# Row traffic of h on POOL's queue, row steps five or six units apart, scores of head pair 6 one unit sooner

## The chip, the cores and the metric

The kernel runs on one core of one Trainium2 chip. The time is the device time of one execution in microseconds, lower being better; the median of three runs is compared. A core has engines that run side by side, each with its own list of instructions in a fixed order: PE multiplies matrices into PSUM, DVE and ACT work on tiles element by element, POOL does a little of that and issues DMAs, and SP only issues DMAs. An instruction waits on semaphores for what it needs, and all that stands behind it on its engine waits too. That holds for DMA issues: what stands on SP behind an issue that waits is not issued.

## The reference

One layer over 256 latent tokens and 256 context tokens with 2048 channels, in float32. Both streams are normalised and modulated, projected by one wide matrix, and go through two branches:

```python
mod = jax.nn.silu(c) @ w_mod[l] + b_mod[l]
shift, scale, gate = jnp.split(mod[:, None, :], 3, axis=-1)
h = _layer_norm(x) * (1.0 + scale) + shift
h_c = _layer_norm(ctx) * (1.0 + scale_c) + shift_c
aq, ak, av, az, bq, bk, bv, bz, bg, mga, mgb = _split_cols(h @ w_in[l])
...
y_a = _neighborhood_attention(aq, ak, av, k_ctx, v_ctx, rpb[l])
y_b, y_b_c = _gla_mixer(bq, bk, bv, bg, bq_c, bk_c, bv_c, bg_c, ...)
out = _merge_branches(y_a, az, y_b, bz, mga, mgb, w_br_a[l], w_br_b[l], w_out[l])
x = _layer_norm(DEEPNORM_ALPHA * x + gate * out, ln_g[l], ln_b[l])
```

The first branch is attention over a window of 16 heads with 64 channels (eight pairs of heads). The second is a gated linear recurrence with four heads of 256 key channels and 512 value channels; the kernel computes it as attention weights of all tokens, multiplied by h, and then by the value weights.

## The kernel before

Each float32 operand of a product is split into two parts, hi and lo, of a shorter format, and a product takes three matmuls (hi with hi, lo with hi, hi with lo). ACT makes hi by a cast, DVE makes lo by a subtraction (`split`, L145). The weights come from HBM in units: one tile of 128 x 1024 (or 128 x 704 for the attention's values), fetched by SP into one of four buffers `raw` (`load`, L154), split into three pairs of buffers `hi` and `lo`, and then used by PE for 24 matmuls. `loads` counts the units, from the first after the start of the program. A call that is to be made at a unit stands in the table `events` under that unit's number; `load` makes it right after the split of that unit. That is how the attention's softmax, its transposes and the work on rows of h are laid between the units.

The program in order of time: about 137 us for the modulation, the normalised and transposed h (`hhi`, `hlo`) and the keys of head pairs 0 to 6 (`kp`). Then three groups of two head pairs: for each pair the query product (`qp`, 2 units), whose PSUM bank is emptied by L483, L484 and L487; then the values (`va`, 8 units of `av`, `value_columns`, L564), whose four PSUM banks are those that the query products of the group leave; beside them scores (`s`, L500), softmax and transposes (`tp`, L530) of both pairs. Then pairs 6 and 7, then keys and queries of the second branch (`bk`, `bq`), its gates (L641) and decays, then `attended` (L780) for two heads at a time, then the gates and output projections up to the end.

`attended` needs h again, with tokens on the partitions: h as rows, in the two parts. These rows, `hrows`, are made meanwhile and put in HBM, in eight blocks of 256 channels (`rows_of_h`, L396). For a block: fetch the modulation columns `sb` (512 KB out of `mods`, spread over all partitions) and the raw rows `xr` (four DMAs of 128 KB); scale them on DVE (eight instructions, L411 and L412); make the hi part in `sb` by ACT and the lo part in `xr` by DVE (`parts`); store both in `hrows`. Both tiles live in two buffers with the tag `staging`, which two more tiles of the second branch use later, `cs` and `wg` (L622, L623). So a block's fetch must wait until the block ahead is stored.

Before, all row DMAs are issued by SP, among the weights. Block n is fetched and scaled at unit 6 + 6n, made into parts a unit later, stored at unit 11 + 6n; the last step, block 7's, would be at unit 48, after `cs` and `wg` have been given the buffers, and so it is done in the first `attended`. POOL's queue carries the copies that bring keys and queries to the other half of the partitions (`kh` L477, `q` L488), and a few loads.

```python
for n in range(8):
    events.setdefault(6 + 6 * n, []).append(lambda dma, sub, n=n: rows_event(n, dma, sub))
```

Of the kernel before, what the change touches and what calls it, by code (L numbers as in the profile page):

```python
# [16 lines left out]
P = 128  # L17
# [11 lines left out]
NEG = -1.0e30  # L29
NC = 4  # L30
HELD = 4
SHARES = (
    ((0, 512, False), (512, 512, True), (1024, 512, False), (1536, 512, False)),
    ((0, 512, False), (512, 256, True), (1024, 512, False), (768, 256, True), (1536, 256, False), (1792, 256, False)),
# [54 lines left out]
def tile_backbone_layer(  # L89
# [34 lines left out]
    def k4(shape, name, dt=F32):  # L124
        return work.tile(shape, dt, tag="k4", name=name, bufs=4)
# [54 lines left out]
    def fetch(dst, src):  # L180
        with tc.issue_after(queued[-1]) if queued else nullcontext():
            queued.append(nc.sync.dma_start(dst, src).ins)
# [203 lines left out]
    def store_modulation():  # L386
        tp = bank("mdt")
        nc.tensor.transpose(tp[:64, :P], mds[:].rearrange("p a b k -> p (a b k)"), ident[:])
        mt = k2([64, P], "mdt")
        nc.vector.tensor_copy(mt[:], tp[:64, :P])  # L390
        nc.sync.dma_start(mods[:].rearrange("a b (k p) -> (a b k) p", p=P), mt[:])

    def staging(shape, name, dt=F32R):
        return const.tile(shape, dt, tag="staging", name=name, bufs=2)

    def rows_of_h(n):  # L396
        sb = staging([P, 2, 2, 256], f"sb{n}")
        xr = staging([P, 2, 4, P], f"xr{n}")
        b, x = sb[:].bitcast(F32), xr[:].bitcast(F32)
        cols = slice(256 * n, 256 * n + 256)  # L400

        def fetch_and_scale(dma, sub):
            with tc.issue_after(dma):
                nc.sync.dma_start(b, mods[:, :, cols].partition_broadcast(P))
                for i in range(4):
                    nc.sync.dma_start(x[:, :, i, :], xin[i, :, cols].rearrange("p (f c) -> p f c", f=2))
            for i in range(4):
                xi, s = x[:, :, i, :], i // 2
                scale, shift = (b[:, m, s, :].rearrange("p (f c) -> p f c", f=2) for m in range(2))
                with tc.issue_after(sub):  # L410
                    nc.vector.scalar_tensor_tensor(xi, xi, mvs[:, i, 0:1], scale, ALU.subtract, ALU.mult)  # L411
                nc.vector.scalar_tensor_tensor(xi, xi, rsn[:, 0, i : i + 1], shift, ALU.mult, ALU.add)  # L412

        def parts(dma, sub):
            with tc.issue_after(sub):
                split(
                    sb[:].rearrange("p a b c -> p (a b c)"),
                    xr[:].rearrange("p a b c -> p (a b c)"),
                    x.rearrange("p a b c -> p (a b c)"),
                )  # L420

        def store(dma, sub):
            with tc.issue_after(dma):
                for part, src in enumerate((b, x)):
                    nc.sync.dma_start(
                        hrows[2 * n : 2 * n + 2, :, part].rearrange("f p j c -> p f (j c)"),
                        src.rearrange("p f a b -> p f (a b)"),
                    )

        return fetch_and_scale, parts, store  # L430

    for n in range(8):
        events.setdefault(6 + 6 * n, []).append(lambda dma, sub, n=n: rows_event(n, dma, sub))

    def rows_event(n, dma, sub):
        fetch, parts, store = rows_of_h(n)
        fetch(dma, sub)
        events.setdefault(7 + 6 * n, []).insert(0, parts)
        events.setdefault(11 + 6 * n, []).insert(0, store)

    store_modulation()


    tri = k2([P, 2, P], "tri")
# [96 lines left out]
    def at(step, *calls):  # L541
        for fn, *args in calls:
            events.setdefault(step, []).append(lambda *_, fn=fn, args=args: fn(*args))
# [64 lines left out]
    f0, s0, t0 = attention(6, *first)  # L608
    f0()
    n = len(loads)  # L610
    at(n + 3, (s0, 0))
    at(n + 5, (s0, 1), (t0, 0))
    second = project_pair(7, q)
    f1, s1, t1 = attention(7, *second)
    at(n + 6, (f1,))
    at(n + 7, (s1, 0), (t0, 1))
    at(n + 9, (s1, 1), (t1, 0), (read_values, 6))
    at(n + 11, (t1, 1))
    at(n + 13, (read_values, 7))


    cs = staging([P, 3, T], "cs", F32)  # L622
    wg = staging([P, 2, 512], "wg")  # L623
    wr = k4([P, 2, 512], "wr")
    bgt = const.tile([P, NH, 2], F32, name="bgt")
    ngt = const.tile([P, 4], F32, name="ngt")
    for t, src in ((cs, rope), (wr, wg2), (bgt, bg2), (ngt, ng)):
        nc.gpsimd.dma_start(t[:], src)
    nc.scalar.copy(wg[:], wr[:])
    lo = slice(64, 128)  # L630
    nc.vector.tensor_tensor(out=wg[lo], in0=wr[lo], in1=wg[lo].bitcast(F32), op=ALU.subtract)
    def rope_of(dst, src, name, eng):
        t = k2([P, 2, T], f"rt_{name}")
        for a in range(2):
# [45 lines left out]
    def queries(h, room=acc):  # L680
        qf = k2([P, 2, T], f"qf{h}")
        for a in range(2):
            bp = room(f"bq{h}{a}")
            project_t(f"bq{h}{a}", bp[:, :T], T, xh, xl)
            nc.scalar.mul(qf[:, a, :], bp[:, :T], 1.0 / 16.0)
        return qf
# [155 lines left out]

    pws = [weights_of(0)]
    kf = keys(0)
    turn_gates()
    decays = gates(0)
    kq = kf, queries(0)
    parts = decayed(0, *decays, *kq)
    decays = gates(1)
    kq = keys(1), queries(1)  # L850
# [373 lines left out]
```

## Time and profile before

| | |
|---|---|
| median of 3 runs | 1245.19 us (1243.39 to 1246.96) |
| the profiled execution | 1247.71 us, of which the span from the first to the last instruction is 1246.0 us |
| mean granted clock of PE | 0.994 |
| DMA | 264.55 MB, mean 212 GB/s |
| queue of SP (q1) | 83744 packets, 252.53 MB |
| queue of POOL (q0) | 4736 packets, 10.37 MB |
| row DMAs | 8 of sb, 32 of xr, 16 of hrows, all issued by SP |

The page of the profile has engines' busy times and their shares of the span; lists of who waited for whom; and, on request, each engine's instructions in order of time. A row of that order has the start in us, the duration, the engine, the line, the tile written and the tile read, and in brackets how long the engine had been idle just ahead of it and what ended that. PE's matmuls overlap, so a start tells more than a duration.

### The profile page before, as it was taken

The numbers are of one execution on the slowest core, as the hardware profiler recorded it, in microseconds if no ns is written. First come the engines' busy times: TensorE is split into PE (matmuls) and PEld (weight loads), VectorE is DVE, ScalarE is ACT, GpSimd is POOL, SyncE is SP. The second block draws the span as 40 slices with busy tenths as digits, with TensorE's granted clock in tenths as the row PEclk, the third lists the DMA queues.
The fourth block names the chain that finished last, engine by engine and source line by source line (L and its number), as shares of the span: only waits on it lengthen the run. The fifth ranks groups of instructions, "written<-read, shape, count | busy, mean of one in ns | idle before, by whom it ended". The sixth has DMA issues, their size and how long they took to land.

```text
span 1246.0 us, 17116 instructions
## 1 busy us (share of the span) xinstructions
PE 1207.7 (97%) x6617; PEld 1015.1 (81%) x6617; DVE 757.5 (61%) x1114; ACT 536.9 (43%) x752; POOL 73.0 (6%) x106
## 2 busy tenths in 40 slices
PE   6999989999999999999999999999999999999997
PEld 5666889989788998888788898788888888888785
DVE  6755566666569376355543368898555554555577
ACT  4322445545456354253533364444444344444440
POOL 1000101010110101002000000000000000000111
PEclk9999989999999999999999999999999999999999
DMA  9997458787743434554645669989655556557661
GB/s 378 418 407 285 145 151 245 186 202 178 216 155 120 134 108 130 203 152 135 233 145 182 215 207 319 312 299 312 210 186 191 196 186 195 194 186 269 223 218 68
DMA packets 88993, 264.55 MB, mean 212 GB/s; under 512 B 9536, under 2 KB 22928, under 8 KB 83792
## 3 DMA queue, kind: packets, MB, share of 16 engines
q1 hardware_dynamic: 83744, 252.53, 60.3%
q0 software_dynamic: 4736, 10.37, 2.9%
q8 instruction: 52, 0.85, 0.3%
q10 hardware_dynamic: 432, 0.56, 0.1%
q14 instruction: 29, 0.24, 0.1%
HBM read 247.66 MB, written 10.52 MB: 207 GB/s over the span
## 4 chain that ended last, share of the span: by engine, by line
PE 70%; DMA 12%; DVE 10%; issue 3%; ACT 3%; SPq 2%; POOL 0%; DVEq 0%; ACTq 0%; POOLq 0%
PE bk L143 7%; PE mgb L143 7%; PE mga L143 7%; PE pb L143 7%; PE g L143 6%; PE o L143 6%; PE kp L143 6%; PE pa L143 3%; DMA wg<-in_wgate 3%; PE va L143 3%; PE bq L143 3%; PE wo L143 3%; PE az L143 2%; DMA hrows<-xr 2%; PE gp L143 2%
## 5 line engine op out<-in xcount | busy, mean ns | idle before, releaser
L149 DVE TENSOR_TENSOR l_wv<-r_wv,h_wv 128x1024 fp32r<-128x1024 f32 x32 | 39.2, 1225 | 79.8 <-ACT h_wv L147 79.6
L143 PE MATMUL o<-h_wv,gt 128*128 128x512 f32 x256 | 84.1, 391 | 0.6 <-DVE gt L149 0.6
L143 PE MATMUL g<-ah,hr 128*128 128x512 f32 x256 | 79.3, 390 | 1.1 <-DMA hr<-hrows 1.1
L143 PE MATMUL va<-h_av,hhi 128*128 128x352 f32 x192 | 64.5, 336 | 9.9 <-ACT q L487 9.9
L149 DVE TENSOR_TENSOR l_pb<-r_pb,h_pb 128x1024 fp32r<-128x1024 f32 x32 | 39.2, 1225 | 47.8 <-ACT h_pb L147 47.8
L147 ACT CAST h_wv<-r_wv 128x1024 fp32r<-128x1024 f32 x32 | 33.6, 1049 | 74.4 <-DMA r_wv<-in_wst 74.4
L143 PE MATMUL va<-h_av,hlo 128*128 128x352 f32 x192 | 63.0, 328 | 0.0
L143 PE MATMUL va<-l_av,hhi 128*128 128x352 f32 x192 | 62.9, 327 | 0.0
L149 DVE TENSOR_TENSOR l_mgb<-r_mgb,h_mgb 128x1024 fp32r<-128x1024 f32 x32 | 39.2, 1224 | 32.7 <-ACT h_mgb L147 32.5
L955 DVE SCALAR_TENSOR_TENSOR gacc<-wg,sc,gacc 128x512 f32<-128x512 f32 x64 | 46.4, 747 | 17.9 <-DMA wg<-in_wgate 17.5
L143 PEld LDWEIGHTS o<-h_wv,gt 128*128 128x128 f32 x256 | 47.8, 188 | 11.6 <-DVE gt L149 1.8
L149 DVE TENSOR_TENSOR l_mga<-r_mga,h_mga 128x1024 fp32r<-128x1024 f32 x32 | 39.1, 1223 | 28.9 <-ACT h_mga L147 28.9
L143 PEld LDWEIGHTS g<-ah,hr 128*128 128x128 f32 x256 | 47.7, 188 | 11.0 <-DMA hr<-hrows 1.3
L147 ACT CAST h_mga<-r_mga 128x1024 fp32r<-128x1024 f32 x32 | 33.8, 1055 | 49.5 <-PE mga L143 31.2
L143 PE MATMUL kp<-hhi,h_ak 128*128 128x512 f32 x128 | 52.7, 418 | 2.2 <-ACT hhi L304 2.2
L147 ACT CAST h_mgb<-r_mgb 128x1024 fp32r<-128x1024 f32 x32 | 33.6, 1054 | 47.7 <-PE mgb L143 26.1
L147 ACT CAST h_pb<-r_pb 128x1024 fp32r<-128x1024 f32 x32 | 33.7, 1053 | 43.4 <-PE pb L143 30.1
L143 PE MATMUL bz<-l_bz,hhi 128*128 128x512 f32 x128 | 50.1, 391 | 2.0 <-DVE l_bz L149 2.0
L143 PE MATMUL kp<-hhi,l_ak 128*128 128x512 f32 x128 | 51.7, 404 | 0.0
L304 ACT ACTIVATE hhi<-xt,mds 128x256 fp32r<-128x256 f32 x32 | 17.5, 594 | 78.8 <-DVE mds L298 78.8
L143 PE MATMUL bk<-hhi,h_bk 128*128 128x512 f32 x128 | 50.4, 394 | 0.7 <-ACT kf L675 0.7
L143 PE MATMUL kp<-hlo,h_ak 128*128 128x512 f32 x128 | 50.6, 398 | 0.0
(351 smaller groups left out, 3560.4 us busy)
## 6 DMA issues: line engine op xcount, KB each, us to landing
wm<-in_wmod SPq DMA_DIRECT2D x32, 1024.0 KB, 9.4
hr<-hrows SPq DMA_DIRECT2D x32, 512.0 KB, 4.3
r_wv<-in_wst SPq DMA_DIRECT2D x32, 512.0 KB, 3.6
r_bz<-in_wst SPq DMA_DIRECT2D x32, 512.0 KB, 4.9
wg<-in_wgate SPq DMA_DIRECT2D x64, 256.0 KB, 5.1
r_mga<-in_wst SPq DMA_DIRECT2D x32, 512.0 KB, 3.6
r_mgb<-in_wst SPq DMA_DIRECT2D x32, 512.0 KB, 3.3
r_pb<-in_wst SPq DMA_DIRECT2D x32, 512.0 KB, 3.3
```

Source lines behind the costliest of these rows:

```text
L143: return nc.tensor.matmul(o, a, b, start=start, stop=stop).ins
L147: cast = nc.scalar.copy(hi, src)
L149: sub = nc.vector.tensor_tensor(out=lo, in0=src, in1=hi.bitcast(F32), op=ALU.subtract)
L304: cast = nc.scalar.activation(hhi[:, s, kt, :], x, AF.Identity, scale=m, bias=b)
L955: nc.vector.scalar_tensor_tensor(part, raw[:], sc[:, n // 4, 0:1], part, ALU.mult, ALU.add)
```

## The change

All row DMAs, and the store of `mods`, are issued on POOL. The fetch of block 0 is issued as soon as `mods` is stored; that of block n + 1 right behind block n's stores, in the same step. The steps are a table, `ROW_STEPS`: scaling at units 6, 11, 17, 22, 27, 32, 37 and 42, parts and stores a unit later. The scaling stands behind the unit's subtraction on DVE without the order that `issue_after` forced. Block 7 is thus finished at unit 43, ahead of `cs` and `wg`, whose loads and splits move behind the first keys of the second branch; the queries of its head 0 are put ahead of its gates. The first scores of head pair 6 come a unit sooner (n + 2), the last transposes and the values of pair 7 a unit later.

```diff
+ROW_STEPS = (6, 11, 17, 22, 27, 32, 37, 42)
...
-        nc.sync.dma_start(mods[:].rearrange("a b (k p) -> (a b k) p", p=P), mt[:])
+        nc.gpsimd.dma_start(mods[:].rearrange("a b (k p) -> (a b k) p", p=P), mt[:])
...
-        def fetch_and_scale(dma, sub):
-            with tc.issue_after(dma):
-                nc.sync.dma_start(b, mods[:, :, cols].partition_broadcast(P))
-                for i in range(4):
-                    nc.sync.dma_start(x[:, :, i, :], xin[i, :, cols].rearrange("p (f c) -> p f c", f=2))
+        nc.gpsimd.dma_start(b, mods[:, :, cols].partition_broadcast(P))
+        for i in range(4):
+            nc.gpsimd.dma_start(x[:, :, i, :], xin[i, :, cols].rearrange("p (f c) -> p f c", f=2))
+
+        def scale(dma, sub):
             for i in range(4):
...
-        def store(dma, sub):
-            with tc.issue_after(dma):
-                for part, src in enumerate((b, x)):
-                    nc.sync.dma_start(
...
+            for part, src in enumerate((b, x)):
+                nc.gpsimd.dma_start(
+                    hrows[2 * n : 2 * n + 2, :, part].rearrange("f p j c -> p f (j c)"),
+                    src.rearrange("p f a b -> p f (a b)"),
+                )
+            if n + 1 < 8:
+                rows_of_h(n + 1)
+
+        events.setdefault(ROW_STEPS[n], []).append(scale)
+        events.setdefault(ROW_STEPS[n] + 1, []).insert(0, parts)
 
     store_modulation()
+    rows_of_h(0)
...
-    at(n + 3, (s0, 0))
+    at(n + 2, (s0, 0))
...
-    at(n + 11, (t1, 1))
-    at(n + 13, (read_values, 7))
+    at(n + 12, (t1, 1))
+    at(n + 14, (read_values, 7))
...
     pws = [weights_of(0)]
     kf = keys(0)
+    cs = staging([P, 3, T], "cs", F32)
+    wg = staging([P, 2, 512], "wg")
...
     turn_gates()
+    qf = queries(0)
     decays = gates(0)
-    kq = kf, queries(0)
+    kq = kf, qf
```

How this moves instructions is seen at three places. The first is SP's list at the values of the first group (r_av is a weight tile on its way into `raw`, rb the attention's bias), before:

```order
L156 DMA r_av_0_1440<-in_wav 128x704
L156 DMA r_av_2_1470<-in_wav 128x704
L404 DMA sb_1476<-mods 128x4x256
L406 DMA xr_1477<-in_xin 128x2x128 x4
L156 DMA r_av_4_1530<-in_wav 128x704
L156 DMA r_av_6_1562<-in_wav 128x704
L156 DMA r_av_8_1619<-in_wav 128x704
L497 DMA rb_1625<-in_rpb 128x768
```

and in the change:

```order
L157 DMA r_av_0_1447<-in_wav 128x704
L157 DMA r_av_2_1477<-in_wav 128x704
L157 DMA r_av_4_1530<-in_wav 128x704
L157 DMA r_av_6_1571<-in_wav 128x704
L157 DMA r_av_8_1628<-in_wav 128x704
L490 DMA rb_1634<-in_rpb 128x768
```

The row fetch no longer stands between the second and the third weight tile of the group.

The second is POOL's list in the third group, from the key copies of pair 5 to those of pair 6, before:

```order
L477 DMA kh_2490<-kn_2486 64x512
L477 DMA kh_2490<-kl_2487 64x512
L488 DMA q_2393<-q_2393 64x256 x4
L477 DMA kh_2980<-kn_2976 64x512 x2
L477 DMA kh_2980<-kl_2977 64x512 x2
```

and in the change, where sb_2312 and xr_2313 are block 4, sb_2553 and xr_2554 block 5, sb_2800 and xr_2801 block 6:

```order
L470 DMA kh_2499<-kn_2495 64x512
L470 DMA kh_2499<-kl_2496 64x512
L423 DMA hrows<-sb_2312 128x2x512
L423 DMA hrows<-xr_2313 128x2x512
L481 DMA q_2404<-q_2404 64x256 x2
L403 DMA sb_2553<-mods 128x4x256
L405 DMA xr_2554<-in_xin 128x2x128 x4
L481 DMA q_2404<-q_2404 64x256 x2
L423 DMA hrows<-sb_2553 128x2x512
L423 DMA hrows<-xr_2554 128x2x512
L403 DMA sb_2800<-mods 128x4x256
L405 DMA xr_2801<-in_xin 128x2x128 x4
```

The query copies of the group's two pairs now stand behind the stores of block 4 and behind the fetch of block 5.

The third is DVE's list at the first scores of pair 4 (s, its bias, its maximum nm, its sum sm and weights pr; xr is the row block's scaling, l_av the lo part of a weight tile), before:

```order
L149 TENSOR_TENSOR l_av_6_2719<-r_av_6_2716,h_av_6_2718 128x704
L508 TENSOR_TENSOR s_0_2645<-s_0_2645,rb_2566 128x2x256
L510 TENSOR_REDUCE nm<-s_0_2645 128x2
L517 RECIPROCAL sm<-sm 128x2
L522 TENSOR_SCALAR pr_0_2653<-pr_0_2653,sm 128x512
L149 TENSOR_TENSOR l_av_8_2776<-r_av_8_2773,h_av_8_2775 128x704
```

and in the change:

```order
L150 TENSOR_TENSOR l_av_6_2728<-r_av_6_2725,h_av_6_2727 128x704
L501 TENSOR_TENSOR s_0_2656<-s_0_2656,rb_2594 128x2x256
L412 SCALAR_TENSOR_TENSOR xr_2554<-xr_2554,mvs,sb_2553 128x2x128
L503 TENSOR_REDUCE nm<-s_0_2656 128x2
L413 SCALAR_TENSOR_TENSOR xr_2554<-xr_2554,rsn,sb_2553 128x2x128
L412 SCALAR_TENSOR_TENSOR xr_2554<-xr_2554,mvs,sb_2553 128x2x128 x2
L413 SCALAR_TENSOR_TENSOR xr_2554<-xr_2554,rsn,sb_2553 128x2x128
L510 RECIPROCAL sm<-sm 128x2
L413 SCALAR_TENSOR_TENSOR xr_2554<-xr_2554,rsn,sb_2553 128x2x128
L515 TENSOR_SCALAR pr_0_2664<-pr_0_2664,sm 128x512
L412 SCALAR_TENSOR_TENSOR xr_2554<-xr_2554,mvs,sb_2553 128x2x128
L150 TENSOR_TENSOR l_av_8_2793<-r_av_8_2790,h_av_8_2792 128x704
```

The scaling of block 5 now stands among the softmax of pair 4, ahead of its maximum.

More of the change, by code (lines that the diff above doesn't have):

```diff
@@ L420, in parts @@
                 )
-        def store(dma, sub):
-            with tc.issue_after(dma):
-                for part, src in enumerate((b, x)):
-                    nc.sync.dma_start(
[L426 to L439, printed above, removed]
+            for part, src in enumerate((b, x)):
[7 more added lines that the diff above has]
+        events.setdefault(ROW_STEPS[n] + 1, []).insert(0, parts)
     store_modulation()
+    rows_of_h(0)
     tri = k2([P, 2, P], "tri")
@@ L617, in tile_backbone_layer @@
     at(n + 9, (s1, 1), (t1, 0), (read_values, 6))
-    at(n + 11, (t1, 1))
-    at(n + 13, (read_values, 7))
[L622 to L631, printed above, removed]
+    at(n + 12, (t1, 1))
+    at(n + 14, (read_values, 7))
     def rope_of(dst, src, name, eng):
@@ L844, in tile_backbone_layer @@
     kf = keys(0)
+    cs = staging([P, 3, T], "cs", F32)
+    wg = staging([P, 2, 512], "wg")
+    wr = k4([P, 2, 512], "wr")
+    bgt = const.tile([P, NH, 2], F32, name="bgt")
+    ngt = const.tile([P, 4], F32, name="ngt")
+    for t, src in ((cs, rope), (wr, wg2), (bgt, bg2), (ngt, ng)):
+        nc.gpsimd.dma_start(t[:], src)
+    nc.scalar.copy(wg[:], wr[:])
+    lo = slice(64, 128)
+    nc.vector.tensor_tensor(out=wg[lo], in0=wr[lo], in1=wg[lo].bitcast(F32), op=ALU.subtract)
     turn_gates()
+    qf = queries(0)
     decays = gates(0)
-    kq = kf, queries(0)
+    kq = kf, qf
     parts = decayed(0, *decays, *kq)
```

## The prediction

> **What bounds the kernel now.** I read the page first, then who waited for whom on PE, then the order of time on SP, ACT, DVE and PE around each of PE's waits, and last the stages.
>
> The page's first part, and the list of PE's waits over the whole span (engine, line, what it waited for: us in total, times, longest):
>
> ```profile
> PE 1207.7 (97%) x6617; PEld 1015.1 (81%) x6617; DVE 757.5 (61%) x1114; ACT 536.9 (43%) x752; POOL 73.0 (6%) x106
> ...
> PE va L143 <- ACT q L487: 9.9, 3, 5.2
> ...
> PE s L143 <- ACT pr L514: 2.6, 1, 2.6
> ...
> PE g L143 <- DMA hr<-hrows: 1.1, 1, 1.1
> ```
>
> PE is the bound: 1207.7 of 1246.0 us, so only 38.3 us are idle. The change can win only what PE loses between the first row block (about 140 us) and the last (about 605 us): three waits of va, 9.9 us; one of s, 2.6; one of g, 1.1.
>
> The first va wait in order of time (start, us, engine and line; brackets: idle before and what ended it), on SP, ACT, DVE and PE:
>
> ```profile
> 144.57 0.44 SPq L404 DMA_DIRECT2D sb<-mods  x1
> 145.06 5.36 SPq L406 DMA_DIRECT2D xr<-in_xin  x4
> 150.51 2.67 SPq L156 DMA_DIRECT2D r_av<-in_wav  x3
> ...
> 158.38 0.78 ACT L147 CAST h_av<-r_av 128x704 fp32r<-128x704 f32 x1 [5.12 <-DMA r_av<-in_wav]
> 160.44 0.38 ACT L487 ACTIVATE q<-qp 64x256 fp32r<-64x256 f32 x1 [0.49 <-DVE q L484]
> ...
> 155.98 0.88 DVE L411 SCALAR_TENSOR_TENSOR xr<-xr,mvs,sb 128x256 f32<-128x256 f32 x2 [4.23 <-DMA xr<-in_xin]
> ...
> 160.87 0.66 PE L143 MATMUL va<-h_av,hhi 128*128 128x352 f32 x1 [5.16 <-ACT q L487]
> 161.33 0.49 PE L143 MATMUL va<-l_av,hhi 128*128 128x352 f32 x1
> 161.63 0.49 PE L143 MATMUL va<-h_av,hlo 128*128 128x352 f32 x1
> ...
> 170.04 0.32 PE L143 MATMUL va<-l_av,hhi 128*128 128x352 f32 x1
> 170.19 0.32 PE L143 MATMUL va<-h_av,hlo 128*128 128x352 f32 x1
> ```
>
> SP issues the row fetch (sb, four xr) ahead of the third weight tile r_av; the four xr take 5.36 us, so r_av leaves at 150.51 and lands about 158.4. ACT, which works in order, sits on its cast for 5.12 us, and the copies L487 that free the PSUM bank of the query product stand behind it, the last at 160.44: PE waits 5.16 us. The other two waits are the same story at the next two groups:
>
> ```profile
> 209.05 2.67 SPq L156 DMA_DIRECT2D r_av<-in_wav  x3
> ...
> 216.52 0.78 ACT L147 CAST h_av<-r_av 128x704 fp32r<-128x704 f32 x1 [5.81 <-DMA r_av<-in_wav]
> ...
> 265.37 1.92 SPq L156 DMA_DIRECT2D r_av<-in_wav  x3
> ...
> 272.69 0.78 ACT L147 CAST h_av<-r_av 128x704 fp32r<-128x704 f32 x1 [6.46 <-DMA r_av<-in_wav]
> ```
>
> A second loss is hidden in busy time. After the 5.2 us wait va matmuls start 0.30 us apart (161.33, 161.63); later 0.15 (170.04, 170.19). The stages of 40 us (PE, PEld, DVE, ACT, POOL busy; granted clock, DMA share, GB/s) show it as the clock:
>
> ```profile
> 160.00:200.00 40.00, 39.13 (x233) 38.07 (x234) 27.38 (x43) 20.49 (x38) 4.58 (x9) 0.91 0.65 183
> 200.00:240.00 40.00, 37.98 (x268) 35.55 (x267) 22.50 (x35) 18.41 (x35) 2.04 (x4) 1.00 0.66 178
> 240.00:280.00 40.00, 37.33 (x258) 34.92 (x257) 28.24 (x47) 19.48 (x36) 6.11 (x12) 0.96 0.88 221
> ```
>
> Lost: 9% and 4% of 40 us, 3.6 + 1.6 = 5.2 us.
>
> **The change part by part.**
>
> *Weights no longer behind rows on SP.* On SP the 57 issues of mods (1), sb (8), xr (32) and hrows (16) go; r_av tiles follow each other (order rows above). r_av can leave when its buffer is free, some 4 us sooner, and lands before ACT's cast. What is late next at the first place: DVE scales the rows with the query's subtractions among them, and from the first scaling (155.98) to the end of the last L487 (160.82) it was 4.8 us. DVE is free at 151.8 (its row of 150.86, below, and 0.89), so the last L487 ends at 156.6; PE stood from 155.7 (160.87 less 5.16): 0.9 us stay. At the other two places the row work moves away from the query's evacuation, or its data are fetched some five units sooner; I leave nothing there. So 9.9 - 0.9 = **9.0 us won**. The clock loss goes with its waits; I leave 1 us: 5.2 - 1.0 = **4.2 us**.
>
> *Row block 7.* Now it finishes before cs and wg take its buffers; before, it was served at 586 to 600 us and g waited on hrows: **1.1 us**, all won.
>
> *Scores of pair 6 a unit sooner.* The wait of 2.6 us was DVE standing on xr:
>
> ```profile
> 319.00 0.36 SPq L404 DMA_DIRECT2D sb<-mods  x1
> ...
> 329.26 0.91 DVE L411 SCALAR_TENSOR_TENSOR xr<-xr,mvs,sb 128x256 f32<-128x256 f32 x2 [3.60 <-DMA xr<-in_xin]
> ...
> 338.21 0.70 DVE L508 TENSOR_TENSOR s<-s,rb 128x512 f32<-128x512 f32 x1
> ```
>
> Now DVE treats s ahead of the row scaling, but xr7 stands before the next weights (l_bk); I take 1.6 of 2.6, **1.6 us won**.
>
> *At no cost.* The turns and values of pair 7 come a unit later, on PE between matmuls that have their weights; what reads them (the gated path, L842) is far off. cs and wr are fetched behind block 7's stores as they were behind block 6's.
>
> Won in all: 9.0 + 4.2 + 1.1 + 1.6 = **15.9 us**.
>
> *What the rows cost on POOL.* POOL's own work is small (73.0 us busy), so issue time is not the matter; the round of one block is, since block n+1 uses block n's two buffers. Its rows (count: min/median/max ns), issues (median us to landing), and a fetch with little beside it (block 7):
>
> ```profile
> L411 DVE SCALAR_TENSOR_TENSOR xr<-xr,mvs,sb x32: 462/479/486, 156.0 to 591.8; 128x256 f32<-128x256 f32 x32
> L147 ACT CAST sb<-xr x8: 1045/1048/1053, 161.0 to 592.9; 128x1024 fp32r<-128x1024 f32 x8
> L149 DVE TENSOR_TENSOR xr<-xr,sb x8: 1219/1224/1226, 162.0 to 594.7; 128x1024 fp32r<-128x1024 f32 x8
> ...
> hrows<-xr SPq DMA_DIRECT2D x8, 512.0 KB, 5.3
> ...
> wr<-in_wg POOLq DMA_DIRECT2D x1, 512.0 KB, 5.2
> ...
> r_bk<-in_wst SPq DMA_DIRECT2D x16, 512.0 KB, 3.7
> ...
> 585.96 1.92 SPq L406 DMA_DIRECT2D xr<-in_xin  x4
> ...
> 589.25 0.48 DVE L411 SCALAR_TENSOR_TENSOR xr<-xr,mvs,sb 128x256 f32<-128x256 f32 x1 [0.77 <-DMA xr<-in_xin]
> ```
>
> Scaling 8 x 0.48 = 3.8, cast 1.05, subtraction 1.2, store 5.3, and a fetch between 3.3 us (585.96 to 589.25, xr alone) and 10.3 (319.00 to 329.26, sb and xr behind other work on SP). That makes 14.7 to 21.7 us. The trace shows no row DMA on POOL; the nearest price of that queue is 512 KB in 5.2 us against 3.7 on SP, 1.5 more a hop, two hops a round: 17.7 to 24.7. I take a fetch of 8 us, between the ends since the queue is its own but the engines are shared (DMA share 0.65 to 0.88): a round of about 22.4.
>
> The time that PE gives for a round: from unit 6 to unit 42 DVE went in before from 150.86 to 324.44:
>
> ```profile
> 150.86 0.89 DVE L149 TENSOR_TENSOR l_av<-r_av,h_av 128x704 fp32r<-128x704 f32 x1 [1.31 <-ACT h_av L147]
> ...
> 324.44 1.22 DVE L149 TENSOR_TENSOR l_aq<-r_aq,h_aq 128x1024 fp32r<-128x1024 f32 x1 [3.56 <-ACT h_aq L147]
> ```
>
> 173.6 us, less the 9.9 and 5.2 lost there, 158.5 over seven gaps: 22.6 us a gap. The round just fits, with nothing to spare, and the gaps are uneven. The shortest is block 5: its store begins after step 28's subtraction, and DVE needs its data right behind s of pair 4 (order rows above: a scaling stands ahead of the nm of s). The two places before:
>
> ```profile
> 257.84 1.22 DVE L149 TENSOR_TENSOR l_aq<-r_aq,h_aq 128x1024 fp32r<-128x1024 f32 x1
> ...
> 278.44 0.70 DVE L508 TENSOR_TENSOR s<-s,rb 128x512 f32<-128x512 f32 x1
> ```
>
> Of these 20.6 us some 4 go (the third va wait and its slow clock), and scaling and subtraction (5.0) come in ahead of the store: some 11.5 are left, when store and fetch want 5.3 + 8, or 3.0 more. It is late by 2 to 5 us; PE has two units of va (24 x 0.16 us each, 7.7 us) before it needs that PSUM pair again, and the chain s, nm, exponentials takes half of these. I put 1.5 us there. The queries' copies q, which now stand behind hrows or sb on POOL, and the four kh, which wait for row DMAs landing, are needed within 10 us: 0.7 us. The gates of head 0, now after its queries, meet DVE later: 0.5 us. **Cost 2.7 us.**
>
> *Sum.* 15.9 - 2.7 = 13.2 us. The profiled execution took 1247.7 (1246.0 span, 1.7 around it): 1234.5 for such a one. It was 2.5 above the median of the three runs, 1245.2, so I forecast a median of **1232**.
>
> A rule that speaks against it: the Trainium skill, "SBUF — State Buffer", section "SBUF: two separate sides", says a DMA issued from GpSimd is starved while VectorE runs a copy that takes both ports, since its descriptors cannot be written; it names 3.1 us in place of 0.62. No row here shows that: POOL's own issues (count: min/median/max ns) are even, with VectorE busy 61%:
>
> ```profile
> L477 POOL DMA_DIRECT2D kh<-kl x16: 512/519/567, 141.1 to 337.8; - x16
> ```
>
> By that rule, an estimate, 2.5 us on each of two hops a round would make the round 27.4 and the time about 1263; by the row it adds nothing, and I go by the row, with a chance for the rival below.
>
> **The rivals.**
>
> *Rows come early.* With a fetch of 5 us or less the round is 19.4, all waits of the cost part go, and of s nothing is left: 15.9 + 1.0 = 16.9 off, and part of the 1.9 left at the first wait and the clock: median 1227. For it: block 7's 3.3 us. Against: DMA share up to 0.88 there, and block 7's row traffic is added to the same stretch.
>
> *Same transfers, same wait.* The weights share the 16 engines with the rows on whatever queue; r_av lands as late as before, or DVE stands on late rows. The round at 24.7 costs (24.7 - 22.6) x 7 = 14.7 of the 15.9: about 1244. For it: DMA share 0.65 to 0.88 where the waits are. Against: r_av was not slow on the engines, it left late (150.51), behind 5.36 us of issues. The Trainium skill, "DMA: Bandwidth & Descriptors", "Issuing engines are not separate DMA queues", says that another issuing engine saves only issue time; the row shows that issue time is just what was lost here.
>
> *Slower.* Row issues on POOL are held up by DVE or by landing waits in one file: POOL issues in order, so q and kh of the next scores stand behind hrows, which stands behind DVE. If each of seven issues of a round is stretched by one DVE copy (0.68 us, the kT copy below), the round is 22.4 + 4.8 = 27.2, and 7 x 4.6 = 32 us are lost against 15.9 won: 1261; at 26 it is 1253. It decides from a round of 24.9 (22.6 + 15.9 / 7).
>
> ```profile
> 139.50 0.68 DVE L458 COPY kT<-kp 128x512 f32<-128x512 f32 x1
> ```
>
> For it: such copies run all through the attention part. Against: the even 512 to 567 ns.
>
> **How the numbers follow.** Forecast 1232 (1228 to 1238): 0.55. Rows early, 1227: 0.20. Same transfers, 1240 to 1248: 0.14. Slower, 1250 to 1262: 0.11. The range leaves out the slower rival and the edge of the third: 1225 to 1246. Faster and slower are counted from 0.3% (3.7 us), about what a measurement can tell: below 1241.5, forecast, early rows and a little of the third, 0.77; above 1248.9, 0.11; between, 0.12.
>
> **What would show it.** In the profile after: va waits on L487 of at most 2 us in all, and a granted clock of 0.98 or more in 160:280 (first terms). ACT's wait for r_av gone; if it is still 5 us, the third rival. DVE's wait for xr: up to 10 us in all if my round is right, near none if rows are early, over 25 if they are slow. No wait of g on hr. The longest new PE wait at s or tp of pair 4 or 5. POOL's issues of xr near 0.5 us; over 1 us, the slower rival. The prediction is wrong if PE's idle between 140 and 620 us does not fall by at least 6 us.

## The result and the profile after

| | before | after |
|---|---|---|
| median | 1245.07 us (6 runs, 1243.39 to 1247.16) | 1251.86 us (6 runs, 1250.58 to 1253.52) |
| after / before | | 1.0054, 95% interval 1.004 to 1.0068 |
| span of the profiled execution | 1246.0 us | 1250.8 us |
| mean granted clock | 0.994 | 0.990 |
| POOL's queue (q0) | 10.37 MB, 2.9% of the 16 engines' time | 27.19 MB, 9.6% |

The change makes the kernel slower by half a per cent; the forecast was a gain of one. PE's waits from 140 to 620 us in the profile after (engine, line, what it waited for: us in total, times, longest):

```profile
PE s L144 <- DMA q<-q: 9.1, 2, 7.5
PE va L144 <- ACT q L480: 7.6, 2, 6.6
PE s L144 <- DVE xr L413: 3.0, 1, 3.0
PE qp L144 <- DVE low L573: 1.7, 1, 1.7
```

Two of the three va waits have all but gone, but the longest has grown from 5.2 to 6.6 us. The wait of s for the softmax weights (2.6) has become two waits for the query's copy (9.1), and two waits are new: s behind the row scaling, and qp behind DVE's emptying of the value banks. In all PE is idle for 23.0 of the 480 us from 140 to 620, where it was idle for 16.6 before. The stages show what the clock takes besides (columns as in the prediction):

```profile
160.00:200.00 40.00, 37.40 (x221) 36.35 (x222) 28.80 (x48) 20.90 (x40) 12.76 (x19) 0.91 0.78 195
...
240.00:280.00 40.00, 39.79 (x284) 37.66 (x283) 25.82 (x40) 20.48 (x37) 16.53 (x26) 1.00 0.99 227
280.00:320.00 40.00, 35.36 (x225) 33.97 (x224) 28.23 (x50) 20.38 (x37) 8.56 (x13) 0.96 0.68 192
320.00:360.00 40.00, 30.94 (x169) 24.75 (x169) 19.45 (x29) 14.26 (x27) 10.02 (x17) 0.87 0.72 185
```

The loss of 240:280 is cured; that of 160:200 stays, and 280:360 is new. ACT's last copy of the second branch's keys says how far PE is behind, before and after:

```profile
573.20 0.59 ACT L675 COPY kf<-bk 128x512 f32<-128x512 f32 x1 [4.34 <-PE bk L143]
```

```profile
584.35 0.59 ACT L658 COPY kf<-bk 128x512 f32<-128x512 f32 x1 [4.34 <-PE bk L144]
```

It is 11.2 us behind there, and 4.8 at the end of the span: the wait of g for hr (1.1) is gone, as are those of o on DVE (0.6) and of bz on its weights (2.0). These are 3.7 of the 6.4 us made up; the rest was not traced.

**The first place.** SP issues no rows any more, and the weight tiles are late all the same (SP, ACT, DVE and PE, each in order of time):

```profile
144.48 5.26 SPq L157 DMA_DIRECT2D r_av<-in_wav  x3
...
156.75 0.78 ACT L148 CAST h_av<-r_av 128x704 fp32r<-128x704 f32 x1 [6.48 <-DMA r_av<-in_wav]
...
158.73 0.78 ACT L148 CAST h_av<-r_av 128x704 fp32r<-128x704 f32 x1 [0.80 <-DMA r_av<-in_wav]
...
158.37 0.87 DVE L412 SCALAR_TENSOR_TENSOR xr<-xr,mvs,sb 128x256 f32<-128x256 f32 x2
...
162.60 0.66 PE L144 MATMUL va<-h_av,hhi 128*128 128x352 f32 x1 [6.60 <-ACT q L480]
```

These are the second, third and fourth weight tile of the group, issued within 5.3 us, and ACT still sits 6.48 us before its cast of the second, which it had not waited for before. The third left at 146.87 in place of 150.51, and ACT has it at 158.73, no sooner than before (158.38). What the transfers took says why. For r_av between 143 and 165 us, before and after:

```profile
DMA to landing us min/median/max: 4.3/7.3/7.8
```

```profile
DMA to landing us min/median/max: 5.1/12.0/12.2
```

And in the stage 144:148 the 16 DMA engines are busy for 0.94 of the time while they move 74 GB/s (last two columns); in 160:200 they moved 195 at 0.78:

```profile
144.00:148.00 4.00, 4.00 (x36) 4.00 (x35) 1.85 (x3) 1.63 (x3) 1.03 (x2) 1.00 0.94 74
```

That is the time of the fetch of sb, which now leaves at 139.78, some 5 us sooner than before (144.57), and lands 11.7 us later. Busy engines that move little are the clue that the experiments followed. It is not the only way in which such a fetch shows: before, with the same fetch on SP's queue, the engines were busy for only 0.26 of the stage 148:152, while SP's four xr issues stretched over 5.36 us:

```profile
148.00:152.00 4.00, 4.00 (x36) 4.00 (x35) 2.21 (x3) 2.09 (x5) 1.03 (x2) 1.00 0.26 88
```

**Block 5 and pair 6.** The fetch of block 5 on POOL, DVE's first scaling of it, and PE's wait behind that:

```profile
270.82 0.80 POOL L403 DMA_DIRECT2D sb<-mods  x1 [3.24 <-DMA hrows<-sb]
...
282.69 0.48 DVE L412 SCALAR_TENSOR_TENSOR xr<-xr,mvs,sb 128x256 f32<-128x256 f32 x1 [5.81 <-DMA sb<-mods]
...
285.91 1.20 PE L144 MATMUL s<-kh,q 128*128 128x512 f32 x4 [2.99 <-DVE xr L413]
```

From the issue to the first scaling it took 11.9 us. And POOL's list at pair 6, with PE's two waits:

```profile
320.11 0.78 POOL L403 DMA_DIRECT2D sb<-mods  x1
...
322.56 0.55 POOL L481 DMA_DIRECT2D q<-q  x1 [1.67 <-DVE q L477]
...
324.27 2.83 POOL L405 DMA_DIRECT2D xr<-in_xin  x4 [1.16 <-DMA hrows<-xr]
...
327.10 0.55 POOL L481 DMA_DIRECT2D q<-q  x1
...
334.10 1.19 PE L144 MATMUL s<-kh,q 128*128 128x512 f32 x2 [7.46 <-DMA q<-q]
336.88 0.76 PE L144 MATMUL s<-kh,q 128*128 128x512 f32 x1 [1.60 <-DMA q<-q]
```

The copies of 64 KB leave at 322.56 and 327.10 and are needed at 326.6 (334.10 less 7.46).

### The profile page after: what moved, and what is told of

The parts are those of the page before. It is cut to its first block, busy times and chain, and to the rows that moved or that the text cites. A ratio compares the mean times of both kernels' runs of the same rounds, so it can differ in the third digit from the quotient of the medians.

```text
span 1250.8 us, 17133 instructions
## 1 busy us (share of the span) xinstructions
PE 1208.2 (97%) x6617; PEld 1016.7 (81%) x6617; DVE 756.9 (61%) x1114; ACT 536.6 (43%) x752; POOL 115.8 (9%) x163
## 3 DMA queue, kind: packets, MB, share of 16 engines
q0 software_dynamic: 9760, 27.19, 9.6%
## 4 chain that ended last, share of the span: by engine, by line
PE 75%; DMA 12%; DVE 7%; issue 4%; ACT 2%; POOL 1%; SPq 0%; DVEq 0%; ACTq 0%; POOLq 0%
PE bk L144 7%; PE bz L144 7%; PE g L144 7%; PE mgb L144 7%; PE mga L144 7%; PE pb L144 7%; PE o L144 7%; PE kp L144 7%; PE bq L144 4%; PE pa L144 3%; PE az L144 3%; PE gp L144 2%; PE wo L144 2%; DMA sb<-mods 2%; DMA r_av<-in_wav 2%
## 5 line engine op out<-in xcount | busy, mean ns | idle before, releaser
L148 ACT CAST h_bz<-r_bz 128x1024 fp32r<-128x1024 f32 x32 | 33.7, 1053 | 38.6 <-PE bz L144 33.8
```

Source lines behind the costliest of these rows:

```text
L148: cast = nc.scalar.copy(hi, src)
```

## The experiments

Three theories at first: (1) POOL's queue works in order, so q stands behind block 7's fetch, and the scores ask for it a unit sooner; (2) the sb fetch on POOL's queue holds the 16 DMA engines, so weights, rows and q are all late; (3) the round of five units is too short. Ratios are to the kernel before, run on the same chip beside each (its median there was 1244.1 to 1246.3 us).

| run | kernel | median, us | ratio, 95% interval |
|---|---|---|---|
| | the change | 1251.86 | 1.0054 (1.0040 to 1.0068) |
| e1 | change, early scores undone | 1249.70 | 1.0034 (1.0013 to 1.0054) |
| e2 | change, q on ACT's queue | 1249.53 | 1.0033 (1.0018 to 1.0049) |
| e3 | before, early scores alone | 1248.63 | 1.0028 (1.0013 to 1.0042) |
| e4 | change, sb on SP's queue | 1253.11 | 1.0054 (1.0037 to 1.0070) |
| e5 | e1, sb filled from x | 1226.84 | 0.9859 (0.9836 to 0.9882) |
| e6 | e1, last row steps later | 1237.14 | 0.9945 (0.9923 to 0.9967) |
| e7 | before, row steps two units later | 1247.47 | 1.0015 (1.0002 to 1.0028) |
| e8 | e1, first fetch and steps later | 1237.18 | 0.9938 (0.9918 to 0.9959) |
| e9 | change, four copies of mods, four fetches | 1230.21 | 0.9872 (0.9838 to 0.9905) |
| e10 | e9, all from one copy | 1229.17 | 0.9871 (0.9841 to 0.9901) |
| e11 | e9, early scores undone | 1224.99 | 0.9835 (0.9805 to 0.9866) |
| e12 | before, four copies, four fetches | 1226.95 | 0.9855 (0.9820 to 0.9891) |
| f1 | change, layout of mods alone | 1231.96 | 0.9902 (0.9884 to 0.9920) |
| f2 | change, four fetches alone | 1246.98 | 1.0014 (1.0002 to 1.0027) |
| f3 | before, layout of mods alone | 1228.42 | 0.9869 (0.9851 to 0.9887) |
| f4 | f1, early scores undone | 1225.12 | 0.9847 (0.9828 to 0.9865) |
| f5 | change, rows of mods 9 KB apart | 1230.26 | 0.9867 (0.9850 to 0.9885) |

### e1: the early scores undone

```diff
-    at(n + 2, (s0, 0))
+    at(n + 3, (s0, 0))
```

> The changed kernel with only the first scores of pair 6 put back to the unit where they stood before. Theory 1 (POOL's queue works in order, so pair 6's last copy q leaves at 327.1 behind block 7's sb and xr, and the scores now ask for it a unit sooner): PE's wait of s on q falls from 9.1 to about 3 us, the granted clock of 320 to 340 us rises from 0.79 to over 0.9, and the time falls by 5 to 8 us, to 1244 to 1247. Rival (the loss comes from the slow row fetch as such, which holds the transfer engines whatever the scores do): the same time is lost a unit later or in block 7's scaling, 1250 to 1252.

The wait of s on q fell from 9.1 to 2.5 us, but a wait of 2.5 for the softmax weights came back. The time fell by about 2 us, less than theory 1 asked, and the two ratios' intervals overlap: in this kernel the early scores are at most a part of the loss. e3 against before, and f1 against f4, show their price more clearly.

### e2: q on ACT's queue

```diff
-            nc.gpsimd.dma_start(ql[o, j, :], ql[r, j, :])
+            nc.scalar.dma_start(ql[o, j, :].bitcast(F32), ql[r, j, :].bitcast(F32))
```

> The changed kernel with the 16 copies q moved from POOL's queue to ACT's, all else kept, the early scores of pair 6 too. Theory 1 (order on POOL's queue): the copy leaves within 1 us of its subtraction, lands in about 6 us, and the wait of s on q nearly goes: 1243 to 1247, less about 1 us for 16 issues on ACT. Theory 2 (the sb fetch on POOL's queue holds the 16 transfer engines, 1.1 us a packet of 4 KB): q leaves early but still lands late, as r_av on SP's queue does now (12.0 us at the first place): s still waits 3 us or more, 1248 to 1251.

The copies left at 320.5 and 322.3, right behind their subtractions, and s still waited for them. PE's two waits, and q from issue to landing between 318 and 336 us:

```profile
331.98 1.19 PE L144 MATMUL s<-kh,q 128*128 128x512 f32 x2 [7.12 <-DMA q<-q]
334.26 0.77 PE L144 MATMUL s<-kh,q 128*128 128x512 f32 x1 [1.09 <-DMA q<-q]
```

```profile
DMA to landing us min/median/max: 11.4/11.6/11.8
```

64 KB took 11.6 us on a queue of their own, while the fetch of block 7 was under way. So POOL's order alone did not make q late; this fits theory 2. The time is some 2 us below that of the change, with intervals that overlap.

### e3: the early scores alone, in the kernel before

```diff
-    at(n + 3, (s0, 0))
+    at(n + 2, (s0, 0))
```

> The kernel before with one part of the change alone: the first scores of pair 6 a unit sooner, no row traffic moved. If the forecast's term is right, the wait of s (2.6 us) shrinks by about 1.6 and the time is 1242 to 1245. Theory 1 says that nothing is wrong with the early scores as long as POOL's queue holds only kh and q: no wait of s on q over 2 us. Rival (the scores are too early by themselves, q needs 6 to 7 us from issue to landing on any day): s waits 3 us or more on q and the time is 1246 to 1249.

With nothing else changed the time rose by 0.28%, as the rival said. The last copy left at 319.35 and landed 8.6 us later:

```profile
328.07 0.76 PE L143 MATMUL s<-kh,q 128*128 128x512 f32 x1 [5.94 <-DMA q<-q]
```

### e4: sb on SP's queue

```diff
-        nc.gpsimd.dma_start(b, mods[:, :, cols].partition_broadcast(P))
+        events.setdefault(ROW_STEPS[n] - 1, []).append(
+            lambda dma, sub: nc.sync.dma_start(b, mods[:, :, cols].partition_broadcast(P))
+        )
```

> The changed kernel with one of its three kinds of row DMA back on SP's queue: the eight sb fetches (modulation columns to all partitions), each issued a load ahead of its scaling; xr, hrows, kh and q stay on POOL's queue. Theory 2 (on POOL's queue sb goes as 128 packets of 4 KB that take up to 1.3 us each and fill the 16 engines for about 10 us; on SP's as 512 packets of 1 KB, 1.5 to 7 us): engine time of sb falls to before's, r_av lands in 7 us instead of 12 at the first place, DVE has no wait of 5.8 us for sb at 282, and the s wait of 3.0 goes: 1240 to 1246. Theory 1 alone (order on POOL's queue): only block 7's sb leaves the way of q, 0.8 us, 1250 to 1252; and SP, which waits for a store to land before it issues sb, may hold weights up: then over 1252.

The gain did not come. DVE waited more for sb (10.0 us in three waits against 5.8 in one), since SP had to wait for the store of the block ahead to land (block 5's left at 275.96, when the store that POOL had issued from 267.64 on had just landed), and sb still took 10.2 us to land, against 11.2 on POOL's queue. So the queue is not what makes this fetch slow.

### e5: sb filled from x

```diff
-        nc.gpsimd.dma_start(b, mods[:, :, cols].partition_broadcast(P))
+        nc.gpsimd.dma_start(b, xin[:, :, cols].rearrange("(m s) p c -> p m s c", m=2))
```

> The kernel of e1 (changed kernel, first scores of pair 6 put back) with sb filled from x itself, so that every partition reads its own four KB in place of all 128 reading the same four; same queue, same bytes, same shape of the descriptors. The rows that come out are scaled with the wrong numbers. Theory 2a (one hot spot in memory: 128 partitions read the same 4 KB): the packets of sb fall from up to 1.3 us to about 0.16, a fetch holds the engines for 1 to 2 us and no longer 10, r_av lands in 4 to 7 us at the first place, DVE waits for no sb, and the time falls by 4 to 9 us below e1's, to 1241 to 1246. Rival 2b (packets of 4 KB on POOL's queue are slow whatever they read, or the fetch is late for another reason): engine time of sb as in the changed kernel, time as e1, 1248 to 1251.

This kernel leaves the modulation out of sb, so its rows are not those of h; it is a probe of time alone. Same queue, same bytes, and 22 us less than e1: no wait over 0.7 us is left between 140 and 620 us, and the clock is 1.00 from 160 to 400. One thing more differs: x is there from the start, so the fetch of block 0 left at 3.39 and no sb flew at the first place at all. The seven other fetches follow the same steps as in e1, and landed in 4.8 to 8.4 us where e1's median is 10.9. The loss hangs on what sb reads. Whether it is the number of readers was not yet told.

### e6, e7, e8: the row steps

```diff
-ROW_STEPS = (6, 11, 17, 22, 27, 32, 37, 42)
+ROW_STEPS = (6, 11, 17, 22, 28, 33, 39, 45)
```

> The kernel of e1 with the last four row steps at 28, 33, 39, 45 in place of 27, 32, 37, 42: blocks 4 to 7 one to three loads later, the round that was too short (block 5) 5 loads again but clear of the scores, the next two 6. Theory 3 (a round of 5 loads is shorter than store and fetch, so DVE stands on sb with the scores behind it): the s wait of 2.9 us, the qp wait of 2.6 and the slow clock after them go, 5 to 8 us less than e1: 1242 to 1245. Rival (these waits come from weights that land late because the engines are full, wherever the scaling stands): within 2 us of e1, 1248 to 1251.

```diff
-        events.setdefault(6 + 6 * n, []).append(lambda dma, sub, n=n: rows_event(n, dma, sub))
+        events.setdefault(8 + 6 * n, []).append(lambda dma, sub, n=n: rows_event(n, dma, sub))
```

(parts and store likewise)

> The kernel before, SP's queue as it was, with every row step two loads later (8 + 6n in place of 6 + 6n, its store as well): the weights r_av of the first group then stand ahead of the row fetch on SP. If the forecast's first term is right (r_av is late because it is issued behind the fetch), the first va wait of 5.2 us goes and the other two shrink, with 3 to 5 us of slow clock: 1234 to 1240. Rival (the fetch slows r_av on the shared engines, or DVE's row work delays the copies of q, wherever the fetch stands): va waits of 6 us or more remain in all, 1242 to 1248.

```diff
-ROW_STEPS = (6, 11, 17, 22, 27, 32, 37, 42)
+ROW_STEPS = (8, 13, 18, 23, 28, 33, 39, 45)
...
-    rows_of_h(0)
+    events.setdefault(5, []).append(lambda dma, sub: rows_of_h(0))
```

> The changed kernel with the scores of pair 6 put back, row steps at 8, 13, 18, 23, 28, 33, 39, 45, and the first row fetch issued on POOL behind the copies q of the first two pairs, after the first weights r_av have been issued, where it stood ahead of them by 5 us. Theory 2 (the slow sb fetch holds the engines while r_av is on its way, 12.0 us to land): r_av lands in 5 to 7 us at the first place, the va wait of 5 to 7 us and its slow clock go, and with the longer rounds of e6 the time is 1236 to 1241. Rival (the copies of q are late because DVE's row work stands before them): the va wait stays over 4 us and the time is as e6's.

e6 gained 12 us on e1, more than expected, though its first va wait stayed (6.3): with a slow fetch the last blocks want longer rounds (four of its seven gaps are six units, where the change has one; block 5's is still five), or scalings that keep clear of the scores; e6 does not tell the two apart. In e7 the va waits went, and the first copy kf<-bk came 13.6 us sooner than before (341.3 against 354.9), so the forecast's first term is there to be won on SP, by keeping the fetch (9.8 us to land, as slow as ever) away from the weight tiles. All of it was lost again when block 7, now at unit 50, held up the first `attended`:

```profile
581.45 0.80 PE L143 MATMUL ap<-near 128*128 128x128 f32 x2 [4.95 <-DVE near L730]
...
594.71 1.19 PE L143 MATMUL g<-ah,hr 128*128 128x512 f32 x2 [7.05 <-DMA hr<-hrows]
```

That is why its time lies in the range of the rival. In e8 the first va wait fell to 2.9, but one of 2.7 came at the second group; in all it gave no more than e6. It is no test of theory 2 at the first place, for its sb was not delayed. POOL's list shows that only xr moved (from 140.59 after the change):

```profile
139.44 0.82 POOL L403 DMA_DIRECT2D sb<-mods  x1 [2.26 <-DMA mods<-mdt]
...
149.68 1.46 POOL L405 DMA_DIRECT2D xr<-in_xin  x2
```

The three weight tiles issued behind that sb still took 8.7 to 9.9 us to land.

### e9 to e12: copies of mods

```diff
+        mp = const.tile([P, 8, 4, 2], F32, name="mp")
+        nc.vector.tensor_copy(mp[:], mds[:].rearrange("p a b (n h) -> p n (a b) h", h=2))
...
-        nc.gpsimd.dma_start(mods[:].rearrange("a b (k p) -> (a b k) p", p=P), mt[:])
+        nc.gpsimd.dma_start(mods[:].rearrange("r q p -> q r p"), mt[:].unsqueeze(1).to_broadcast([64, 4, P]))
...
-        nc.gpsimd.dma_start(b, mods[:, :, cols].partition_broadcast(P))
+        for r in range(4):
+            w = P // 4
+            nc.gpsimd.dma_start(
+                b[w * r : w * r + w].rearrange("p m s c -> p (m s c)"),
+                mods[r, 8 * n : 8 * n + 8, :].rearrange("q p -> (q p)").partition_broadcast(w),
+            )
```

> The changed kernel, early scores of pair 6 kept, with the modulation columns stored four times in memory (one store, 128 KB) and sb fetched as four DMAs of 32 partitions, each from a copy of its own; a block's columns lie together, so a partition reads 4 KB in one piece. One small copy on DVE more. Theory 2a (128 readers of the same 4 KB): with 32 readers of a copy the fetch holds the engines for half as long or less, and most of the 23 us between e1 and e5 comes back: 1228 to 1238, of which 3 to 4 us stay lost to the early scores. Rival 2c (e5 was fast only because x lay elsewhere, or four more issues and the file of POOL's landings cost what the copies save): 1245 to 1252.

> The kernel of e9, copies, layout and four DMAs kept, but all four read the first copy. Theory 2a: the hot spot is back, sb's packets take about 1 us again and the time is that of the changed kernel, 1248 to 1256. Rival (the layout in one piece of 4 KB, or the cut into four DMAs, is what helps): the time is that of e9 within 3 us.

> The kernel of e9 with the first scores of pair 6 put back: both causes taken away, the right result kept. With theories 1 and 2a the time comes near e5's 1226.8, some way above it for the 32 readers left: 1227 to 1235, and under e9's by 2 to 5 us. Rival (without the slow fetch the copies q are in time, so the early scores cost nothing): within 1 us of e9.

> The kernel before, all on SP's queue, with the same four copies and four fetches. If the fetch of 10.3 us that the forecast took as the upper end was the hot spot there too (1.5 to 7.0 us of engine time a block), the three va waits and the s wait shrink in part: 1238 to 1243. Rival (on SP's queue r_av is late for its place behind the fetch's issues, not for the fetch's length; three more issues a block): 1244 to 1249.

e9 gave 1230, inside the range of theory 2a, but for another reason: e10, where all partitions read one copy, gave the same, and the number of readers (theory 2a) falls. e11 was, with f4 below, the fastest kernel of all, and e12 did nearly as much for the kernel before, on SP's queue, far more than was expected of it. What e9 and e10 share is the layout (a block's 4 KB in one piece) and the cut into four.

### f1 to f5: what in the layout

```diff
-    mods = dram.tile([2, 2, D], F32, name="mods")
+    mods = dram.tile([64, P], F32, name="mods")
...
-        nc.gpsimd.dma_start(b, mods[:, :, cols].partition_broadcast(P))
+        nc.gpsimd.dma_start(
+            b.rearrange("p m s c -> p (m s c)"),
+            mods[8 * n : 8 * n + 8, :].rearrange("q p -> (q p)").partition_broadcast(P),
+        )
```

(f1, f4; f3 the same on SP. The small copy mp of e9 stands ahead of the transpose.)

> The changed kernel with one thing different: the modulation columns lie block by block in memory, so that the 4 KB that a block needs are one piece and not four of 1 KB that are 8 KB apart. One copy, one DMA of 128 partitions, as before. Theory 2d (the four pieces at a distance of 8 KB are what makes the packets slow): as e9 and e10, 1227 to 1232. Theory 2e (the cut into four DMAs did it): as the changed kernel, 1249 to 1254.

```diff
-        nc.gpsimd.dma_start(b, mods[:, :, cols].partition_broadcast(P))
+        for r in range(4):
+            w = P // 4
+            nc.gpsimd.dma_start(b[w * r : w * r + w], mods[:, :, cols].partition_broadcast(w))
```

> The changed kernel, its layout of the modulation columns kept, with sb fetched as four DMAs of 32 partitions from POOL's queue. Theory 2d (layout): packets of sb still take about 1 us, 1248 to 1256. Theory 2e (cut): 1227 to 1232.

> The kernel before, all row traffic on SP's queue, with the layout of f1. By theory 2d the three va waits and the s wait go as in e12 (four copies, four fetches): 1225 to 1230. By 2e: 1243 to 1247. If the forecast's first term were right in itself (weights behind the row issues on SP cost 9 us of waits whatever the fetch takes), 6 us or more of va waits would remain: 1234 to 1240.

> f1 with the first scores of pair 6 put back: the changed kernel's queue, the short fetch, no early scores. By theories 1 and 2d near e11: 1223 to 1227, some 2 to 5 us under f1 and 0 to 4 us under f3, which is then all that the move from SP's queue to POOL's is worth. Rival (with one DMA of 128 partitions the fetch is slower than in e11): 1228 to 1235.

```diff
-    mods = dram.tile([2, 2, D], F32, name="mods")
+    mods = dram.tile([2, 2, D + 256], F32, name="mods")
```

(f5; its store of mods is four DMAs, one a row)

> The changed kernel with the four rows of the modulation columns 9 KB apart in memory in place of 8 KB (each row 256 numbers longer than its data; the store of mods becomes four DMAs). A block is still read as four pieces of 1 KB by all 128 partitions. If the distance of 8 KB is what makes it slow, the time is near f1's: 1229 to 1236. If it is the four pieces by many readers, it is the changed kernel's: 1248 to 1254.

The layout does it (f1, f3, f4); the cut alone saves about 5 us (f2). And f5, which still reads four pieces of 1 KB but with rows 9 KB apart in place of 8, is as fast as f1. The fetch itself, issues of sb with the median us to landing in the last column, before, after the change, in e5, in f1 and in f5:

```profile
sb<-mods SPq DMA_DIRECT2D x8, 512.0 KB, 10.4
sb<-mods POOLq DMA_DIRECT2D x8, 512.0 KB, 11.2
sb<-in_xin POOLq DMA_DIRECT2D x8, 512.0 KB, 6.3
sb<-mods POOLq DMA_DIRECT2D x8, 512.0 KB, 5.0
sb<-mods POOLq DMA_DIRECT2D x8, 512.0 KB, 5.5
```

The profile of f1 in the stage that moved 74 GB/s after the change, and r_av there between 143 and 165 us:

```profile
144.00:148.00 4.00, 4.00 (x35) 4.00 (x35) 1.88 (x2) 1.43 (x3) 2.85 (x6) 1.00 0.88 256
```

```profile
DMA to landing us min/median/max: 3.5/5.4/6.8
```

In POOL's queue the same 27.19 MB in the same 9760 packets take 7.1% of the 16 engines' time in f1 and 9.6% after the change (after first):

```profile
q0 software_dynamic: 9760, 27.19, 9.6%
```

```profile
q0 software_dynamic: 9760, 27.19, 7.1%
```

Of spans of 1250.8 and 1230.0 us these are 120.1 and 87.3 us; the difference is 4.1 us of all engines for each of the eight blocks. In f3 SP's list is ordered as before, and even its issues are short: the four xr take 2.19 us where they took 5.36:

```profile
145.19 2.19 SPq L411 DMA_DIRECT2D xr<-in_xin  x4
147.42 4.81 SPq L156 DMA_DIRECT2D r_av<-in_wav  x3
```

Its va waits add up to 0.2 us.

## Why the prediction was wrong, step by step

**Weights no longer behind rows on SP, 9.0 won: wrong in size.** The step that failed is "r_av can leave when its buffer is free, some 4 us sooner, and lands before ACT's cast". The third tile left 3.6 us sooner, took some 12 us to land, and came no sooner than before; the second, left at 144.48, took as long and came later than before. Of 9.9 us of va waits 7.6 stayed. The trace of before had shown a fetch that held up whatever was issued near it, and the prediction put all of that down to SP's issue time. Its argument that "r_av was not slow on the engines, it left late" did not hold even there: the third tile took 7.8 us to land, where the second, issued ahead of the fetch, took 4.3 (the row of r_av before, above). In f3 the order on SP is untouched and the waits are gone: the 5.36 us of issues were themselves the slow fetch showing. The rival "same transfers, same wait" named this mechanism, though at a smaller price, and its sign came true: ACT's wait for r_av, 6.48 us, was still over 5.

**The clock, 4.2 won: wrong.** It goes with the long waits. 160:200, with one of 6.6 us, stayed at 0.91; 280:320 and 320:360, with 3.0 and 9.1, came to 0.96 and 0.87; 240:280 lost its wait of 2.7 and rose from 0.96 to 1.00. Not each wait costs clock: before, 320:360 had one of 2.6 at 1.00.

**Scores of pair 6, 1.6 won: wrong sign.** The prediction looked at DVE, which freed s, and never set the landing of q against the unit that the scores moved to, though q's median of 7.1 us from issue to landing stood in before's list of DMA issues. e3 shows this part losing 0.28% by itself. On the other side, f1 to f4, it costs 6.8 us, and there POOL's order has a share: f1's last q leaves at 311.10, right behind four xr that were issued from 308.26 on.

**A fetch of 8 us, a round of 22.4: the mis-sized term.** "I take a fetch of 8 us, between the ends"; block 5's took 11.9, above even the upper end of 10.3. The lower end, 3.3, was xr alone: block 7's sb had left at 545.01, some 40 us ahead of it, so the slow part was not in it. Before's list of DMA issues had the medians, 10.4 us for sb and 9.0 for xr. The extra 1.5 us a hop that the prediction put on POOL's queue is not there for the stores: hrows landed in 3.9 and 5.0 us, against 4.6 and 5.3 on SP. For the fetch it is about 1 us (sb 11.2 against 10.4, xr 10.1 against 9.0). The place was right (block 5, s of pair 4), at 3.0 us of wait for the 1.5 forecast, with the clock of 280:320 on top.

**Block 7, 1.1 won: right.** g no longer waits for hr. That more was made up behind 584 us was not foreseen.

**The slower rival** had the time (1250 to 1262), not the reason; that the time fell into its range is chance. POOL's issues were not stretched by DVE (busy us, mean ns):

```profile
L405 POOL DMA_DIRECT2D xr<-in_xin x32 | 22.7, 713 | 8.0 <-DMA hrows<-xr 8.0
...
L470 POOL DMA_DIRECT2D kh<-kn x16 | 8.5, 535 | 23.7 <-ACT ya L551 19.8 <-ACT kn L148 2.4 <-PE tp L523 0.6
L470 POOL DMA_DIRECT2D kh<-kl x16 | 8.4, 526 | 19.0 <-DMA sb<-mods 16.0 <-DMA xr<-in_xin 1.8 <-DVE kl L150 0.8
```

The key copies take 535 and 526 ns in the mean, within the 512 to 567 of before, so the Trainium skill's rule on starved descriptors ("SBUF — State Buffer", "SBUF: two separate sides") is not seen here either, with POOL issuing 57 DMAs more. Its second half, one file for all, is seen: the key copies stood for 16.0 us in all until an sb had landed. But PE waited for no key copy, and what q loses by standing behind rows is small: e2 took q out of the file and gained about 2 us, no more than the intervals leave open.

With the slow fetch gone, the forecast's gain from the queue can be read: f4 against f3, on one chip, is 1225.1 against 1228.4 (1224.5 to 1226.4, and 1227.4 to 1228.7), and e11 against e12, on another, is 1225.0 against 1227.0. The ratios' intervals overlap in both pairs. f4 and e11 also have other row steps than f3 and e12, so the whole move to POOL is worth 2 or 3 us, and how much of that is the queue is not shown. The fix that counts is the layout: 1.3% on the kernel before, without any move.

## What to carry to other kernels

When the DMA engines are busy and the rate is a third of what it is elsewhere, or when a queue's issues stretch while the engines idle, find the transfer that is slow before moving it to another queue: here the slow transfer was as slow on another queue, and slowed what flew beside it. A work step may be moved ahead only as far as its last input lands; read issue to landing, not issue alone. Where many partitions read the same few rows of memory, try laying what one transfer needs in one piece, or padding the rows: here 9 KB apart was fast and 8 KB slow.

## What the runs showed of the hardware

- All 128 partitions reading the same four pieces of 1 KB that lie 8 KB apart is slow: 10.4 us to land on SP's queue, 11.2 on POOL's. With 9 KB between them it is 5.5 (f5), and 5.0 with one piece of 4 KB (f1). The same number of bytes from x, where each partition reads pieces of its own, took 6.3 (e5), though x's rows are 8 KB long as well; there neighbouring partitions read 8 KB apart, and the four pieces of one partition lie 1 MB apart. So 128 readers alone do not make it slow, nor does a distance of 8 KB between what different partitions read. Four pieces 8 KB apart with one reader each, and distances other than 8 and 9 KB, were not run. What in the memory is behind it no trace here shows.
- The Trainium skill, "DMA: Bandwidth & Descriptors", "Latency and other measured facts", tells of a loss with large row pitches that are powers of two (from 207 GB/s at 512 KiB down to 103 at 4 MiB), and advises a few KiB of padding or a contiguous layout. Its pitch lies between partitions, the one here between the four pieces that every partition reads. These runs agree in kind and show a loss at 8 KB, where 1 KB of padding was enough.
- The slow fetch is not slow for itself alone: r_av went from 4.1 us (f1, median of 24) to 6.5 after the change, and pair 6's copies q of 64 KB took 11.6 us on a queue of their own (e2).
